# The second product of a decoder MLP by one level of Strassen's rule, in a phase of its own behind the first product

## The chip, the cores and the metric

The kernel runs on one core of a Trainium2 chip, in one launch. The metric is the device time of an execution in microseconds (us); three runs of the kernel before took 2086.72, 2089.35 and 2091.54 us, with 2089.35 as their median. A core has TensorE (PE: matrix products, whose weights are loaded by PEld), VectorE (DVE), ScalarE (ACT), GpSimd (POOL), SyncE (SP, which here issues nearly all transfers) and 16 DMA engines between the device memory (DRAM) and the on-chip memory (SBUF). Products are summed in PSUM, eight banks of 128 x 512 numbers.

## The reference

One decoder layer on 512 tokens of 2048 features, in float32. Three mixers share one input projection; the part that matters here is the end:

```python
x = x + gate1 * (concat[A, B, C] @ W_out)
x = x + gate2 * squared-ReLU MLP(adaLN(RMSNorm(x), c))
# A final RMSNorm is applied after the last layer.
D_MODEL = 2048; SEQ = 512; DEPTH = 1; D_FF = 4 * D_MODEL

def rms_norm(x, g):
    xf = x.astype(jnp.float32)
    y = xf * lax.rsqrt(jnp.mean(xf * xf, axis=-1, keepdims=True) + EPS)
    return (y * g.astype(jnp.float32)).astype(x.dtype)
```

The MLP's first product is 512 x 2048 by 2048 x 8192, then ReLU and a square; its second product is 512 x 8192 by 8192 x 2048. gate2 and the scales and shifts of adaLN are products of the vector c with the matrix ada_w.

## The kernel before

Every float32 product is made of float32r parts: each factor is split into a high part (a cast) and a low part (the factor less its high part), and three matmuls (high by high, low by high, high by low) stand for one. A matmul has a 128 x 128 stationary factor and a moving factor of 512 columns, so it yields 128 x 512 numbers.

Weights come as pieces of 128 x 512 (256 KB). The class Stream loads them on SP's queue in the order of use (L91, tile w_raw), ScalarE casts them (L104, w_hi) and VectorE makes the low part (L105, w_lo), three buffers each. The order in which its calls stand sets the order of the work; all queues are in order.

The first product of the MLP has 64 hidden tiles of 128 features by 512 tokens. Tiles 0 to 6 are made at once, with seven PSUM banks, while norm 2 is still under way; each of the other 57 is 16 pieces' worth of matmuls, 48, in four pieces (L258 to L260, ps_m). Behind a tile, hidden() applies ReLU (L852, ACT), squares (L856, DVE) and splits into m_hi (L857, ACT) and m_lo (L858, DVE). During the tiles behind the seventh, x1 (the residual) is transposed block by block (L842), copied (L844, tile x1t, two buffers) and written to x1_dram (x_dram in the profile).

The second product runs along with the first: mlp2(c) takes chunk c of four hidden tiles, two chunks behind mlp1. For each of four column quarters q it does four hidden tiles by four token blocks by three matmuls into four PSUM banks (L900 to L902, ps_d), 192 matmuls per chunk, and VectorE adds each bank into the sums acc (L892; chunk 0 is a copy on ScalarE). Chunk 14 multiplies by gate2 (g2row) and adds x1. The last chunk, mlp2_last, runs token block by token block (ps_e), and behind each block come squares (L937), the final gain (L938), the sum of squares (L940), one over the root with a Newton step (L304 to L310), the scaling (L947 on DVE, L945 on ACT) and the writes to out.

ada_w, 2 x 1024 columns a piece, is dotted with c on VectorE (L211) between other work, up to the first tiles of the MLP; it loads in transfers of 1 MB or 512 KB on the same SP queue.

## Time and profile before

| | |
|---|---|
| runs | 2086.72, 2089.35, 2091.54 us |
| profiled execution's span | 2089.8 us |
| PE busy | 2062.8 us, 99% |
| DVE busy | 1272.5 us, 61% |
| ACT busy | 776.5 us, 37% |
| DMA, mean | 155 GB/s, 323 MB |

The span of the profiled execution is its own time and stands 0.5 us from the median of the runs. Shares of busy time are averages over all stages. TensorE's busy time is modelled from the starts of its matmuls, so 99% says that there is nearly always one under way. Idle time of an engine counts only where TensorE waits for it.

### The profile page before, as it was taken

The page shows a single profiled execution, that of the slowest core. Times are in us where ns is not written, and L with a number is a line of the kernel's source. Part 1 is how long each engine was busy: PE and PEld are TensorE (multiplying, and loading weights), DVE is VectorE, ACT ScalarE, POOL GpSimd, SP SyncE. Part 2 cuts the span into 40 slices and gives each one's busy share as a digit, 9 for nine tenths or more (in the row PEclk, how much of TensorE's full clock was granted, in tenths as well). Part 3 has the DMA queues.
Part 4 walks back from the last instruction along what each step waited for, and adds up shares of the span by engine and source line. Part 5 has one row for each costly group of instructions (what it writes and reads, how often), then busy time and mean ns, then how long its engine had stood idle before and what let it go on. Part 6 is the DMA issues. An engine that isn't in the chain of part 4 may idle for free.

```text
span 2089.8 us, 26292 instructions
## 1 busy us (share of the span) xinstructions
PE 2062.8 (99%) x9525; PEld 1698.8 (81%) x9525; DVE 1272.5 (61%) x2225; ACT 776.5 (37%) x1433; POOL 3.8 (0%) x12
## 2 busy tenths in 40 slices
PE   9999999999999999999999999999999999999998
PEld 7889877778888887888888888888888888888786
DVE  8998878788977973445544434444344443444687
ACT  4435357766323554323222232222322223222323
POOL 0000000000000000000000000000000000000000
PEclk9999999999999999999999999999999999999999
DMA  9895855546894355545333333333333333333552
GB/s 389 285 318 155 256 161 175 177 155 233 301 341 137 94 190 186 155 117 178 120 116 96 96 97 101 96 96 96 97 100 96 96 91 96 97 98 98 152 161 91
DMA packets 145378, 323.44 MB, mean 155 GB/s; under 512 B 16120, under 2 KB 26944, under 8 KB 138720
## 3 DMA queue, kind: packets, MB, share of 16 engines
q1 hardware_dynamic: 143376, 319.00, 48.6%
q10 hardware_dynamic: 1824, 2.65, 0.4%
q8 instruction: 75, 1.23, 0.2%
q14 instruction: 55, 0.45, 0.1%
q0 software_dynamic: 48, 0.11, 0.0%
...
## 4 chain that ended last, share of the span: by engine, by line
PE 92%; DMA 3%; DVE 3%; issue 1%; ACT 1%; SPq 0%; ACTq 0%; DVEq 0%
PE ps_m L258 11%; PE ps_m L260 11%; PE ps_m L259 11%; PE ps_d L900 10%; PE ps_d L901 10%; PE ps_d L902 10%; PE ps_w L259 3%; PE ps_w L258 3%; PE ps_w L260 3%; PE ps_y L258 1%; PE ps_y L259 1%; PE ps_y L260 1%; PE ps_x L258 1%; PE ps_x L259 1%; PE ps_x L260 1%; DMA w_raw<-in_w 1%
## 5 line engine op out<-in xcount | busy, mean ns | idle before, releaser
L105 DVE TENSOR_TENSOR w_lo<-w_raw,w_hi 128x512 fp32r<-128x512 f32 (+2 forms) x732 | 492.7, 676 | 689.1 <-ACT w_hi L104 678.4
L104 ACT CAST w_hi<-w_raw 128x512 fp32r<-128x512 f32 (+2 forms) x732 | 444.9, 610 | 1066.3 <-PE ps_d L902 432.6
L900 PE MATMUL ps_d<-w_hi,m_hi 128*128 128x512 f32 x960 | 374.6, 391 | 4.1 <-DVE acc L892 2.2
L901 PE MATMUL ps_d<-w_lo,m_hi 128*128 128x512 f32 x960 | 374.4, 390 | 0.0
L902 PE MATMUL ps_d<-w_hi,m_lo 128*128 128x512 f32 x960 | 373.7, 390 | 0.0
L258 PE MATMUL ps_m<-h_hi,w_hi 128*128 128x512 f32 x912 | 356.5, 391 | 0.0
L260 PE MATMUL ps_m<-h_hi,w_lo 128*128 128x512 f32 x912 | 355.1, 389 | 0.0
L259 PE MATMUL ps_m<-h_lo,w_hi 128*128 128x512 f32 x912 | 354.8, 389 | 0.0
L211 DVE SCALAR_TENSOR_TENSOR ada<-ada,crow 128x1024 f32<-128x1024 f32 (+1 forms) x176 | 229.5, 1317 | 11.8 <-DMA ada<-in_ada_w 11.3
L900 PEld LDWEIGHTS ps_d<-w_hi,m_hi 128*128 128x128 f32 x960 | 180.6, 188 | 44.6 <-DVE acc L892 2.6
L902 PEld LDWEIGHTS ps_d<-w_hi,m_lo 128*128 128x128 f32 x960 | 180.6, 188 | 37.6
L901 PEld LDWEIGHTS ps_d<-w_lo,m_hi 128*128 128x128 f32 x960 | 180.5, 188 | 37.3 <-DVE w_lo L105 0.2
L260 PEld LDWEIGHTS ps_m<-h_hi,w_lo 128*128 128x128 f32 x912 | 171.2, 188 | 35.9
L258 PEld LDWEIGHTS ps_m<-h_hi,w_hi 128*128 128x128 f32 x912 | 171.2, 188 | 35.2
L259 PEld LDWEIGHTS ps_m<-h_lo,w_hi 128*128 128x128 f32 x912 | 171.3, 188 | 35.1
L892 DVE TENSOR_TENSOR acc<-acc,ps_d 128x512 f32<-128x512 f32 x224 | 139.6, 680 | 1.8 <-PE ps_d L902 1.8
L858 DVE TENSOR_TENSOR m_lo<-m_t,m_hi 128x512 fp32r<-128x512 f32 x64 | 44.2, 691 | 40.7 <-ACT m_hi L857 40.5
L857 ACT CAST m_hi<-m_t 128x512 fp32r<-128x512 f32 x64 | 39.7, 620 | 47.2 <-DVE m_t L856 47.2
L259 PE MATMUL ps_y<-h_lo,w_hi 128*128 128x512 f32 x128 | 50.0, 390 | 0.8 <-DVE h_lo L337 0.8
L259 PE MATMUL ps_w<-mixc_lo,w_hi 128*128 128x512 f32 x128 | 49.9, 390 | 0.0
L260 PE MATMUL ps_y<-h_hi,w_lo 128*128 128x512 f32 x128 | 49.8, 389 | 0.0
L258 PE MATMUL ps_w<-mixc_hi,w_hi 128*128 128x512 f32 x128 | 49.8, 389 | 0.0
...
## 6 DMA issues: line engine op xcount, KB each, us to landing
w_raw<-in_w SPq DMA_DIRECT2D x668, 256.0 KB, 2.7
ada<-in_ada_w SPq DMA_DIRECT2D x50, 1024.0 KB, 7.1
ada<-in_ada_w SPq DMA_DIRECT2D x92, 512.0 KB, 4.8
...
xT<-in_xT SPq DMA_DIRECT2D x16, 256.0 KB, 7.1
qT<-in_w SPq DMA_DIRECT2D x16, 256.0 KB, 2.8
row<-acs_dram SPq DMA_DIRECT2D x16, 256.0 KB, 3.6
xin<-in_xT SPq DMA_DIRECT2D x16, 256.0 KB, 4.5
```

Of the source, the lines that this page charges most:

```text
L104: self.split = nc.scalar.copy(hi, raw)
L105: self.in_order(lambda: nc.vector.tensor_sub(lo, raw, hi.bitcast(F32)))
L211: return V.scalar_tensor_tensor(w, w, 0.5, crow[:, sl], ALU.mult, ALU.mult, accum_out=acc[:, n:n + 1])
L258: PE.matmul(ps, lhsT=wh, rhs=pair[0], start=first, stop=False)
L259: PE.matmul(ps, lhsT=wh, rhs=pair[1], start=False, stop=False)
L260: PE.matmul(ps, lhsT=wl, rhs=pair[0], start=False, stop=last)
L857: S.copy(hi, t)
L858: V.tensor_sub(lo, t, hi.bitcast(F32))
L892: V.tensor_add(dst, dst, banks[t])
L900: PE.matmul(ps, lhsT=hid[0][:, ts], rhs=w[0], start=first, stop=False)
L901: PE.matmul(ps, lhsT=hid[0][:, ts], rhs=w[1], start=False, stop=False)
L902: PE.matmul(ps, lhsT=hid[1][:, ts], rhs=w[0], start=False, stop=last)
```

## The change

The two products of the MLP become two phases.

In the first phase all 64 hidden tiles are made, one after the other. Hidden tiles n and n + 1 (n even) form a pair; their 512 tokens are cut in halves of 256, which gives the four blocks a11, a21, a12, a22 of Strassen's rule (in Winograd's form). Four subtractions make the other left factors; all seven (128 x 7 x 256) are cast to hx_hi and hx_lo and written to hid_dram, two transfers of 0.92 MB per pair, 64 in all. Only the first product's weights go through Stream here; add_pieces finds where the second product's weights lie in DRAM.

In the second phase the pools of the first are closed. For two column halves p, eight chunks c of four pairs of hidden tiles and seven products m (in the order 2, 4, 3, 6, 5, 1, 7) there is a right factor: a block of weights b11, b21, b22 or b12 (128 x 4 x 512, loaded in two transfers of 512 KB) or one of four sums of blocks, made in place on VectorE. It is split into v_hi and v_lo, and the left factor hs comes back from hid_dram in one transfer of 1 MB. A product is 24 matmuls into a PSUM tile of two banks, of which there are four. VectorE adds it into one of seven sums (128 x 2 x 512). After the eighth chunk the sums are combined into four result blocks, multiplied by gate2, x1 is added, and the final norm follows.

```diff
-        hi = mlp.tile([P, T], F32R, tag="m_hi", bufs=12, name=f"m_hi{f}")
-        lo = mlp.tile([P, T], F32R, tag="m_lo", bufs=12, name=f"m_lo{f}")
-    def mlp2(c, hid):
...
-    def mlp2_last(hid):
...
-    hid = [mlp1(c) for c in range(lead)]
-    for c in range(nchunk - 1):
-        if c + lead < nchunk:
-            hid.append(mlp1(c + lead))
...
-        mlp2(c, hid[c])
-    mlp2_last(hid[-1])
+    for n in range(NFT):
...
+        if n % 2 == 0:
+            x = mlp.tile([P, 7, HT], F32, tag="hx", bufs=2, name=f"hx{n // 2}")
+            relu2(halves(x, 0), ps, cols)
+            continue
+        relu2(halves(x, 5), ps, cols)
+        a11, a21, a12, a22 = x[:, 0], x[:, 1], x[:, 5], x[:, 6]
+        V.tensor_sub(x[:, 2], a12, a22)
+        V.tensor_sub(a12, a12, a11)
+        V.tensor_sub(x[:, 3], a22, a12)
+        V.tensor_sub(x[:, 4], a21, x[:, 3])
+        hi = mlp.tile([P, 7, HT], F32R, tag="hx_hi", bufs=2, name=f"hx_hi{n // 2}")
+        lo = mlp.tile([P, 7, HT], F32R, tag="hx_lo", bufs=2, name=f"hx_lo{n // 2}")
+        S.copy(hi, x)
+        V.tensor_sub(lo, x, hi.bitcast(F32))
+        for part, y in enumerate((hi, lo)):
+            nc.sync.dma_start(hid_dram[n // (2 * KP)][:, :, part, n // 2 % KP].rearrange("i p t -> p i t"), y.bitcast(F32))
...
+    order = (2, 4, 3, 6, 5, 1, 7)
+    def right_factors(p, c):
+        b = []
+        for i, k in enumerate(("11", "21", "22", "12")):
+            b.append(w2_tile(f"b{k}_{p}_{c}"))
+            for half in range(2):
...
+                nc.sync.dma_start(b[-1][:, 2 * half:2 * half + 2], w)
+            if i < 3:
+                yield b[-1]
+        b11, b21, b22, b12 = b
+        q = w2_tile(f"q{p}_{c}")
+        V.tensor_add(q, b11, b12)
+        yield q
+        V.tensor_add(b12, b12, b22)
+        yield b12
+        V.tensor_add(b11, b11, b12)
+        yield b11
+        V.tensor_add(b21, b21, b11)
+        yield b21
...
+                    hs = hs_pool.tile([P, 2, KP, HT], F32R, tag="hs", bufs=3, name=f"hs{p}_{c}_{i}")
+                    nc.sync.dma_start(hs.bitcast(F32), hid_dram[c][i])
+                    hi = wp.tile([P, KP, T], F32R, tag="hi", bufs=3, name=f"v_hi{p}_{c}_{i}")
+                    lo = wp.tile([P, KP, T], F32R, tag="lo", bufs=3, name=f"v_lo{p}_{c}_{i}")
+                    S.copy(hi, raw)
+                    V.tensor_sub(lo, raw, hi.bitcast(F32))
...
+        for k in range(KP):
+            PE.matmul(ps, lhsT=hs[:, 0, k, ts], rhs=hi[:, k], start=(k == 0), stop=False)
+            PE.matmul(ps, lhsT=hs[:, 1, k, ts], rhs=hi[:, k], start=False, stop=False)
+        for k in range(KP):
+            PE.matmul(ps, lhsT=hs[:, 0, k, ts], rhs=lo[:, k], start=False, stop=(k == KP - 1))
...
+    ahead = [next(todo), next(todo)]
+    for _ in range(2 * NCK * 7):
+        p, c, m, hs, hi, lo = ahead.pop(0)
...
+        if c == 0:
+            sums[m] = late.tile([P, 2, T], F32, tag="sum", bufs=11, name=f"sum{p}_{m}")
+            S.copy(sums[m], ps)
+        else:
+            add(sums[m], ps)
...
+        if m == 4:
+            add(sums[7], sums[4])
+            add(sums[4], sums[2])
+            residual(1, 2 * p, sums[4])
+            squares(1, 2 * p)
...
+        elif m == 1:
+            add(sums[7], sums[1])
+            add(sums[6], sums[1])
+            residual(1, 2 * p + 1, sums[6])
+            squares(1, 2 * p + 1)
+            if p:
+                for t in range(2):
+                    write_out(1, t)
+                residual(0, 2, sums[7])
```

residual() multiplies a result block of 128 x 1024 by gate2 and adds x1 (two VectorE operations, L1003 and L1004), squares() makes two squares on ScalarE and two products with the final gain on VectorE (L1012), and write_out() does what stood behind a token block before. In the second column half the last product m = 7 is followed token block by token block.

Three places show how the change moves the work. In the rows a name ends in a running number; of v_lo0_4_6 the figures are column half, chunk and slot of the left factor, of ps_d0_4_2 column half, chunk and product.

VectorE in the middle of the second product, before (chunk 8, where it alternates between splitting weights and adding PSUM banks):

```order
L105 TENSOR_TENSOR w_lo534_13089<-w_raw_534_13086,w_hi534_13088 128x512
L105 TENSOR_TENSOR w_lo535_13107<-w_raw_535_13104,w_hi535_13106 128x512
L105 TENSOR_TENSOR w_lo536_13125<-w_raw_536_13122,w_hi536_13124 128x512
L105 TENSOR_TENSOR w_lo537_13143<-w_raw_537_13140,w_hi537_13142 128x512
L892 TENSOR_TENSOR acc2_7898<-acc2_7898,ps_d8_2_0_13082 128x512
L892 TENSOR_TENSOR acc2_7898<-acc2_7898,ps_d8_2_1_13083 128x512
L892 TENSOR_TENSOR acc2_7898<-acc2_7898,ps_d8_2_2_13084 128x512
L892 TENSOR_TENSOR acc2_7898<-acc2_7898,ps_d8_2_3_13085 128x512
```

The same place in the changed kernel (column half 0, chunk 4):

```order
L984 TENSOR_TENSOR v_lo0_4_1_12934<-b11_0_4_12928,v_hi0_4_1_12933 128x2048
L964 TENSOR_TENSOR q0_4_13036<-b11_0_4_12928,b12_0_4_13033 128x2048
L1029 TENSOR_TENSOR sum0_1_12237<-sum0_1_12237,ps_d0_3_1_12937 128x1024
L984 TENSOR_TENSOR v_lo0_4_6_12969<-b21_0_4_12963,v_hi0_4_6_12968 128x2048
L966 TENSOR_TENSOR b12_0_4_13033<-b12_0_4_13033,b22_0_4_12998 128x2048
L1029 TENSOR_TENSOR sum0_7_12273<-sum0_7_12273,ps_d0_3_7_12972 128x1024
L984 TENSOR_TENSOR v_lo0_4_5_13004<-b22_0_4_12998,v_hi0_4_5_13003 128x2048
L968 TENSOR_TENSOR b11_0_4_12928<-b11_0_4_12928,b12_0_4_13033 128x2048
L1029 TENSOR_TENSOR sum0_2_12061<-sum0_2_12061,ps_d0_4_2_13007 128x1024
L984 TENSOR_TENSOR v_lo0_4_4_13041<-q0_4_13036,v_hi0_4_4_13040 128x2048
L970 TENSOR_TENSOR b21_0_4_12963<-b21_0_4_12963,b11_0_4_12928 128x2048
L1029 TENSOR_TENSOR sum0_4_12099<-sum0_4_12099,ps_d0_4_4_13044 128x1024
```

Operations are four times as long, and additions that make right factors (q, b12, b11, b21) stand between the splits and the sums.

SP's queue where the last weights of the first product are loaded, before (nothing but weights):

```order
L91 DMA w_raw_679_16008<-in_w 128x512
L91 DMA w_raw_680_16026<-in_w 128x512
L91 DMA w_raw_681_16044<-in_w 128x512
L91 DMA w_raw_682_16070<-in_w 128x512
L91 DMA w_raw_683_16088<-in_w 128x512
L91 DMA w_raw_684_16106<-in_w 128x512
```

The same place in the changed kernel, where the phases meet:

```order
L125 DMA w_raw_474_11920<-in_w 128x512
L919 DMA hid_dram7_7129<-hx_hi30_11837 128x7x256
L125 DMA w_raw_475_11938<-in_w 128x512
L919 DMA hid_dram7_7129<-hx_lo30_11838 128x7x256
L959 DMA b11_0_0_12009<-in_w 128x2x512 x2
L959 DMA b21_0_0_12018<-in_w 128x2x512
L919 DMA hid_dram7_7129<-hx_hi31_11986 128x7x256
L919 DMA hid_dram7_7129<-hx_lo31_11987 128x7x256
L959 DMA b21_0_0_12018<-in_w 128x2x512
L959 DMA b22_0_0_12027<-in_w 128x2x512 x2
L959 DMA b12_0_0_12063<-in_w 128x2x512 x2
L980 DMA hs0_0_4_12068<-hid_dram0_7122 128x2048
```

The loads of the first group's weights b21, b22 and b12 stand behind the writes of the last pair's left factors (hx_hi31, hx_lo31).

VectorE at the end of the program, before (the last token block):

```order
L935 TENSOR_TENSOR acc3_7979<-acc3_7979,ps_e3_3_17268 128x512
L938 TENSOR_TENSOR acc3_7979<-acc3_7979,frow_14227 128x512
L940 TENSOR_REDUCE fin3_17212<-fin3_17212 128x1
L304 TENSOR_SCALAR fin3_17212<-fin3_17212 128x1
L306 RECIPROCAL fin3_17212<-fin3_17212 128x1
L307 TENSOR_TENSOR fin3_17212<-fin3_17212 128x1
L308 TENSOR_TENSOR fin3_17212<-fin3_17212 128x1
L309 TENSOR_SCALAR fin3_17212<-fin3_17212 128x1
L310 TENSOR_TENSOR fin3_17212<-fin3_17212 128x1
L947 TENSOR_SCALAR acc0_7736<-acc0_7736,fin3_17212 128x512
L947 TENSOR_SCALAR acc2_7898<-acc2_7898,fin3_17212 128x512
```

In the changed kernel, from the sum of the last product but one on (46 rows end the program from there; these are the first):

```order
L1029 TENSOR_TENSOR sum1_1_14243<-sum1_1_14243,ps_d1_7_1_15924 128x1024
L1003 TENSOR_TENSOR sum1_3_14139<-sum1_3_14139,g2row_13480 128x1024
L1029 TENSOR_TENSOR sum1_7_14279<-sum1_7_14279,sum1_1_14243 128x1024
L1004 TENSOR_TENSOR sum1_3_14139<-sum1_3_14139,x1in0_3_15914 128x1024
L1029 TENSOR_TENSOR sum1_6_14173<-sum1_6_14173,sum1_1_14243 128x1024
L1012 TENSOR_TENSOR sum1_3_14139<-sum1_3_14139,frow_13501 128x512 x2
L1003 TENSOR_TENSOR sum1_6_14173<-sum1_6_14173,g2row_13480 128x1024
L1003 TENSOR_TENSOR sum1_7_14279<-sum1_7_14279,g2row_13480 128x1024
L1004 TENSOR_TENSOR sum1_6_14173<-sum1_6_14173,x1in1_3_15952 128x1024
L1004 TENSOR_TENSOR sum1_7_14279<-sum1_7_14279,x1in0_2_15994 128x1024
L1012 TENSOR_TENSOR sum1_6_14173<-sum1_6_14173,frow_13501 128x512 x2
L1017 TENSOR_REDUCE fin_12008<-fin_12008 128x1 x2
```

What was spread over four token blocks now stands behind the last two products.

## Rows read from the trace of the kernel before

**Rows 1.** The page's head: span, busy time by engine, TensorE's clock in 40 slices.
```profile
span 2089.8 us, 26292 instructions
...
PE 2062.8 (99%) x9525; PEld 1698.8 (81%) x9525; DVE 1272.5 (61%) x2225; ACT 776.5 (37%) x1433; POOL 3.8 (0%) x12
...
PEclk9999999999999999999999999999999999999999
```
**Rows 2.** By line, TensorE: operation, shapes, count | busy us, mean ns | idle before.
```profile
L900 PE MATMUL ps_d<-w_hi,m_hi 128*128 128x512 f32 x960 | 374.6, 391 | 4.1 <-DVE acc L892 2.2 <-ACT x1t L844 1.8
```
**Rows 3.** Timeline of TensorE in the MLP: start us, us, operation.
```profile
1394.98 0.39 PE L258 MATMUL ps_m<-h_hi,w_hi 128*128 128x512 f32 x1
...
1397.70 0.39 PE L258 MATMUL ps_m<-h_hi,w_hi 128*128 128x512 f32 x1
```
**Rows 4.** By line and shape, VectorE and ScalarE, the whole span.
```profile
L752 DVE TENSOR_TENSOR xs<-xs,ps_rms_c 128x2048 f32<-128x2048 f32 x2 | 4.6, 2285 | 1.9 <-PE ps_rms_c L321 1.9
...
L211 DVE SCALAR_TENSOR_TENSOR ada<-ada,crow 128x1024 f32<-128x1024 f32 x160 | 192.9, 1220 | 11.7 <-DMA ada<-in_ada_w 11.3
...
L462 DVE SCALAR_TENSOR_TENSOR gva<-gva,va 128x256 f32<-128x256 f32 x8 | 3.2, 419 | 0.0
...
L104 ACT CAST w_hi<-w_raw 128x512 fp32r<-128x512 f32 x668 | 414.5, 621 | 1017.4 <-PE ps_d L902 432.6 <-PE ps_m L259 379.4 <-PE ps_w L259 81.9
...
L104 ACT CAST w_hi<-w_raw 128x384 fp32r<-128x384 f32 x48 | 24.5, 511 | 36.3 <-PE ps_m L259 11.1 <-PE ps_tm L502 8.2 <-issue 6.0
...
L852 ACT ACTIVATE m_t<-ps_m 128x512 f32<-128x512 f32 x57 | 33.7, 591 | 0.0
...
L844 ACT COPY x1t<-ps_x1t 128x512 f32<-128x512 f32 x16 | 9.3, 584 | 12.5 <-DMA x_dram<-x1t 12.4
```
**Rows 5.** Timeline of VectorE in the beginning of the MLP.
```profile
745.61 0.68 DVE L856 TENSOR_TENSOR m_t<-m_t 128x512 f32<-128x512 f32 x1
746.21 0.69 DVE L854 TENSOR_TENSOR m_t<-ps_m,r 128x512 f32<-128x512 f32 x1
...
763.49 1.22 DVE L211 SCALAR_TENSOR_TENSOR ada<-ada,crow 128x1024 f32<-128x1024 f32 x1
764.63 0.68 DVE L858 TENSOR_TENSOR m_lo<-m_t,m_hi 128x512 fp32r<-128x512 f32 x1
```
**Rows 6.** Windows: us; PE, PEld, DVE, ACT, POOL busy; PE clock; DMA share; GB/s.
```profile
10.00:20.00 10.00, 10.00 (x33) 8.20 (x33) 9.82 (x18) 4.73 (x9) 0.00 (x0) 1.00 1.04 419
...
785.00:795.00 10.00, 10.00 (x52) 8.21 (x51) 5.86 (x10) 4.08 (x8) 0.00 (x0) 1.00 0.93 301
...
805.00:815.00 10.00, 8.24 (x32) 6.28 (x31) 2.68 (x4) 2.84 (x5) 0.00 (x0) 0.83 0.53 187
...
1000.00:1800.00 800.00, 800.00 (x3546) 662.83 (x3545) 338.92 (x523) 224.83 (x369) 0.00 (x0) 1.00 0.35 99
```
**Rows 7.** DMA issues: out<-in, queue, count, KB each, median us to landing.
```profile
ada<-in_ada_w SPq DMA_DIRECT2D x50, 1024.0 KB, 7.1
ada<-in_ada_w SPq DMA_DIRECT2D x92, 512.0 KB, 4.8
...
x_dram<-x1t SPq DMA_DIRECT2D x16, 256.0 KB, 5.1
```
**Rows 8.** Timeline of TensorE where the transposes of x1 wait.
```profile
809.77 0.50 PE L900 MATMUL ps_d<-w_hi,m_hi 128*128 128x512 f32 x1 [1.76 <-ACT x1t L844]
```
**Rows 9.** Timeline of TensorE and VectorE at the end of the span.
```profile
2079.99 0.39 PE L902 MATMUL ps_e<-w_hi,m_lo 128*128 128x512 f32 x1
...
2083.55 0.16 DVE L308 TENSOR_TENSOR fin<-fin 128x1 f32<-128x1 f32 x1
2083.75 0.15 DVE L309 TENSOR_SCALAR fin<-fin 128x1 f32<-128x1 f32 x1
...
2084.13 0.88 DVE L947 TENSOR_SCALAR acc<-acc,fin 128x512 f32<-128x512 f32 x2
```

More of the change, by code (lines that the diff above doesn't have):

```diff
@@ L63, with add_pieces, up, up4 @@
 ROW, ROW_N = _slots([("dt_bias", 16), ("a_log", 16), ("attn_sinks", 16), ("gm_bs", 512)])
+def add_pieces(stream, sizes):
+    offs = [0]
+    for n in sizes:
+        offs.append(offs[-1] + n * P)
+    count = [0, {}]
+    def up(n):
+        for _ in range(n):
+            stream.add(sizes[count[0]], offs[count[0]])
+            count[0] += 1
+    def up4(c):
+        up(4 * len(range(max(7, 4 * c), 4 * c + 4)))
+    def down(c):
+        for q in range(4):
+            for f in range(4 * c, 4 * c + 4):
+                count[1][q, f] = offs[count[0]]
+                count[0] += 1
+    last = NFT // 4 - 1
+    up(len(sizes) - 4 * (NFT - 7) - 4 * NFT)
+    up4(0)
+    up4(1)
+    for c in range(last):
+        if c + 2 <= last:
+            up4(c + 2)
+        down(c)
+    down(last)
+    return count[1]
 def mix_rows():
@@ L899, in mms2 @@
[L899 to L913 removed]
+            V.tensor_mul(dst, ps, r2)
@@ new lines, in prepared @@
+    def prepared():
+        for p in range(2):
+            for c in range(NCK):
+                for m, raw in zip(order, right_factors(p, c)):
+                    i = slot[m]
+                    hs = hs_pool.tile([P, 2, KP, HT], F32R, tag="hs", bufs=3, name=f"hs{p}_{c}_{i}")
[4 more added lines that the diff above has]
+                    V.tensor_sub(lo, raw, hi.bitcast(F32))
+                    yield p, c, m, hs, hi, lo
@@ new lines, in add, with sub @@
+    def add(d, s):
+        V.tensor_add(d, d, s)
+    def sub(d, s):
+        V.tensor_sub(d, d, s)
+    sums = {}
+    todo = prepared()
+    ahead = [next(todo), next(todo)]
+    for _ in range(2 * NCK * 7):
+        p, c, m, hs, hi, lo = ahead.pop(0)
+        if (p, c, m) == (0, NCK - 2, order[0]):
+            g2row, frow = final_rows()
+        ahead += [x for x in (next(todo, None),) if x]
+        ps = psum.tile([P, 2, T], F32, tag="m", bufs=4, name=f"ps_d{p}_{c}_{m}")
+        last = c == NCK - 1
+        for t in range(2):
+            product(ps[:, t], hs, hi, lo, t)
+            if last and p and m == 7:
+                d = sums[7]
+                y = late.tile([P, T], F32, tag="sq", bufs=2, name=f"fin_y{t}")
+                V.tensor_mul(y, ps[:, t], g2row[:, 2])
+                V.tensor_add(d[:, t], d[:, t], y)
+                squares(0, 2, (t,))
+                write_out(0, t)
+        if last and p and m == 7:
+            break
+        if c == 0:
+            sums[m] = late.tile([P, 2, T], F32, tag="sum", bufs=11, name=f"sum{p}_{m}")
+            S.copy(sums[m], ps)
+        else:
+            add(sums[m], ps)
+        if not last:
+            continue
+        if m == 4:
[3 more added lines that the diff above has]
+            squares(1, 2 * p)
+        elif m == 6:
+            add(sums[6], sums[3])
+            sub(sums[6], sums[2])
+        elif m == 5:
+            sub(sums[7], sums[5])
+            add(sums[3], sums[5])
+            residual(0, 2 * p + 1, sums[3])
+            squares(0, 2 * p + 1)
+        elif m == 1:
[4 more added lines that the diff above has]
+            if p:
+                for t in range(2):
+                    write_out(1, t)
+                residual(0, 2, sums[7])
+        elif m == 7:
+            residual(0, 0, sums[7])
+            squares(0, 0)
```

197 lines of the change are left out of this document (86 added, 111 removed).

## The prediction

> **What bounds the kernel now.** I read the head of the page first: TensorE is busy 2062.8 of 2089.8 us [rows 1], and its clock row shows the high level in all 40 slices [rows 1]. The view by line comes next: the second product's 960 matmuls of the first part waited 4.1 us altogether, 2.2 of that for VectorE's additions into acc [rows 2]. So the time is the number of matmuls by their pitch, plus what lies ahead of the first and behind the last. The pitch stands in the timeline: two matmuls 12 places apart start at 1394.98 and 1397.70, so 2.72 / 12 = 0.2267 us (the 0.39 in the rows is one matmul's passage, pipelined with the next) [rows 3]. I then looked at what each helper has to spare, since the change trades matmuls for work on VectorE, ScalarE and the DMA queues.
>
> **Removed.** Before, the second product has 16 chunks of 192 matmuls, 3072. After, 2 column halves by 8 chunks by 7 products of 24 matmuls, 2688. The size of each (128x512) stays, so 384 x 0.2267 = **-87.0 us**. The 2.2 us of waiting for acc goes too: four PSUM buffers of two banks stand between a product and its sum: **-2.2**.
>
> **Added: VectorE in the second phase.** A product lasts 24 x 0.2267 = 5.44 us, a group of seven 38.1, all 16 groups 609 (against 696 before). VectorE gets seven subtractions and four additions of 128x2048 and seven sums of 128x1024 per group. Their durations: 2285 and 1220 ns [rows 4]. Behind one another they cost less: 128x512 operations of 0.68 start 0.60 apart, and the next starts 1.14 after one of 1.22 [rows 5]; so I take 2.20 (an estimate, 2.285 less the same 0.08) and 1.14. A group is 11 x 2.20 + 7 x 1.14 = 32.2 of 38.1 us. ScalarE casts 128x2048 seven times: 128x384 took 511 ns and 128x512 621 [rows 4], a slope of 0.86 ns an element, so about 1.94 us (an estimate), 13.6 us per group. Both are prepared two products ahead in three buffers, so TensorE covers them: **0**. What it costs if the cover fails is rival B.
>
> The Trainium skill ("VectorE: DVE Perf Modes", section "The DRAIN you can't avoid") says that VectorE's next operation does not start before the pipe of the one ahead is empty. The rows disagree here, with starts 0.60 apart for 0.68 us [rows 5]. By the rule a group would be 33.7 us, still inside 38.1, and the ends worked out below some 3 us longer, which would give 2037.
>
> **Added: DMA.** Phase 2 reads 112 left factors of 1.05 MB and 67 MB of weights, 184.5 MB in 609 us: 303 GB/s. The queues carried 419 GB/s at full share in 10 to 20 us and 301 at 0.93 in 785 to 795 [rows 6]; in the MLP 99 GB/s took a share of 0.35, which is 285 GB/s at full share if it scales [rows 6]. These bounds lie on both sides of 303. I take the high one, as rows of 2 and 8 KB (like those loads of ada_w) are what phase 2 moves: **0**. A left factor is asked for when its buffer's product three places earlier ends, and so has 10.9 us; a 1 MB load landed after 7.1 and 512 KB after 4.8 in the crowded beginning [rows 7]. Phase 1 writes two times 0.92 MB per pair of hidden tiles, 21.8 us, beside eight weight pieces of 0.26 MB: 181 GB/s, below any bound: **0** in its steady part. At its beginning the first eight such writes fall where ada_w still loads and shares reach 0.93 [rows 6]; there the write of x1 (12.4 us of waiting for it at L844 [rows 4]) had already held TensorE 1.76 us [rows 8], after which a stretch of ten microseconds had TensorE busy for 8.24 at a granted clock of 0.83, between its two levels, 1.2 and 2.4 GHz [rows 6]. Bounds: this stall goes (-3.5, the 1.76 and the slower clock behind it), or the eight writes are exposed at their 7.4 MB / 301 GB/s = 25 us. I take **+3**, near the stall that is there already.
>
> **Added: the boundary of the phases.** Clock from the end of the last matmul of phase 1: ReLU 0.59 [rows 4], square 0.60, four subtractions of 128x256 at 419 ns [rows 4] to about 3.1; cast of 128x1792 by the slope above, 1.72, to 4.9. The cast of the right factor of the first group's second weight quarter stands behind it on ScalarE (its place is that of the last hidden operand): 6.8 with its 1.94. TensorE's preloaded first product covers nothing before its own right factor is split, whose place comes free at 0 as well; so TensorE idles about 6.9 us. On SP the second half of b21 and all of b22 and b12 stand behind the two writes of the last pair, which wait until 4.9 and 6.9; b21 lands about 13, b22 16, b12 18 (0.5 to 1 MB each at 300 to 400 GB/s). Behind that, four additions and the splits follow at VectorE's pace, and the first group ends about 47.5 instead of 38.1: **+10**, with 7 (only the idle) and 20 (loads at a third of the speed and TensorE at its lower clock behind them) as bounds.
>
> **Added: change of the column half.** The last group of the first half carries extra sums, residuals and squares on VectorE: 8 of 128x1024 for sums and 8 for residuals, 8 of 128x512, 16 x 1.14 + 8 x 0.60 = 23 us on top of 32.2, in 38.1 us. That is 17 too much; two products ahead (10.9) and the slack of the next group (5.9) take it nearly up. I take **+5**, as the splits stand between these in one in-order queue; bounds 0 and 12.
>
> **The end.** Before, the last matmul starts at 2079.99 and the span ends 2089.8: 9.4 us behind PE's end [rows 9]. After, count from the last group's first product's end; the products end every 5.44, the one before the last at 27.2, the last at 32.6. VectorE keeps pace until 27.2 and then has (the order's rows from sum1_1 on) nine operations of 128x1024 at 1.14 (10.3), ten of 128x512 at 0.60 (6.0), eight scalings of 0.44 (0.88 for two) [rows 9] (3.5) and 28 tiny ones at 0.19 (2083.55 to 2083.75) [rows 9] (5.3): 25.1, to 52.3. The last scaling ended 2085.0 before and the span 4.8 later [rows 9]: 57.1, so 24.5 us behind PE's end: **+15** (12 if the small ones overlap, 22 if VectorE is already late at 27.2).
>
> **Sum.** -87.0 - 2.2 + 3 + 10 + 5 + 15 = -56. The profiled execution's span of 2089.8 equals the median of the runs (2089.35) within 0.5 us, so I take 2089.8 - 56 = **2034 us**. With all low bounds (-3.5, 7, 0, 12) it is 2016, with all but the exposed writes at their high ones (3, 20, 12, 22) 2058.
>
> **Rivals.**
> A. *The queues bound phase 2.* At the 285 GB/s of the MLP [rows 6], 184.5 MB take 647 us, 38 more than 609: 2072. For: that rate is from the same weights in the same 2 KB rows. Against: a share scaled up is not a rate seen, and 394 to 419 were. Slower than before only below about 278 GB/s. 15%.
> B. *TensorE waits for the right factors.* This one ends on the other side. The cast, the subtraction and the additions of one product are a chain (b11 needs b12, b21 needs b11), and VectorE's in-order queue puts a sum, which waits for the end of a product, between them. If each product then exposed its cast and the lost overlap, a group lasts 7 x (5.44 + 1.1) = 45.8 us, 16 groups 733: 2034 + 123 = 2157. The point from which it decides: a group above 38.1 + 56 / 16 = 41.6 us. With VectorE merely taking 40 us, +30: 2064. For: VectorE is at 85% with in-order waits. Against: the two-product lead of 10.9 us against a longest VectorE block of 2.20 + 2.20 + 1.14 = 5.5. 10% for the version that is slower, 8% for that at 2064.
> C. *The writes of the left factors in 1 KB rows fill the queues in phase 1.* They are 58.7 MB; if they moved at a third of 301 GB/s, a pair's 1.84 MB would take 18.4 of its 21.8 us and its 2.1 MB of weights another 7.0: 3.6 us over by 28 pairs, +101: 2135, slower. Against: no row shows a write so slow; x1's 256 KB landed after 5.1 us in the median on a crowded queue [rows 7]. 3%.
> The forecast holds the other 64%.
>
> **How the numbers follow.** About 0.2% is what a measurement of this kernel tells from no change, 4 us. Faster: the forecast 64, A 14 of 15, the mild B 8: 86%. Slower: B 10, C 2, a bit of A: 12%. Within: 2%. The forecast's own range is 2016 to 2058; A and the mild B, at 2064 and 2072, are taken in: 2015 to 2075, and left out is some 17%.
>
> **What would show it.** 2688 matmuls in the second phase at 0.227 us and a granted clock at its high level bear out the first term. In the first stretch of ten microseconds of phase 2 TensorE should be busy for some 3, its idle put down to the cast of a right factor and to DMA b22 or b12. In the steady part a group should repeat every 38.1 us, with VectorE busy 33 of it and DMA near 300 GB/s. If its matmuls wait there for v_lo, it is B; if they wait for hs or the raw weights, A; if matmuls of the first product wait for w_lo with DMA named behind, C. Behind the last matmul some 24 us of VectorE should stand. Wrong it is altogether if the group takes over 41.6 us.

## The result, and the profile after

The changed kernel took 2040.49 us (median of four runs, 2036.87 to 2043.13) where the kernel before, in the same session, took 2088.70: a ratio of 0.9765 with the interval 0.9751 to 0.9778, 48 us less. Forecast were 2034 in a range of 2015 to 2075. The profiled execution's span is 2041.4, so the two profiles differ by 48.4 us, and the terms below are counted on them.

The page's head after it, for [rows 1]: TensorE has 79 us less to do, VectorE 265 more, and the clock row shows its first lower slice at the very end.

```profile
span 2041.4 us, 25012 instructions
...
PE 1983.8 (97%) x9141; PEld 1628.7 (80%) x9141; DVE 1537.5 (75%) x2086; ACT 847.8 (42%) x1253; POOL 3.8 (0%) x12
...
PEclk9999999999999999999999999999999999999997
```

The second product's matmuls, for [rows 2] and [rows 3]. By line, the first group of matmuls (L991) now waits 21.0 us, all of it in five waits at the three seams shown below. In the timeline two blocks of 12 matmuls start 2.72 us apart, 0.2267 each as before, and two groups of seven products 38.08 apart.

```profile
L991 PE MATMUL ps_d<-v_hi,hs 128*128 128x512 f32 x896 | 351.3, 392 | 21.0 <-DVE fin L337 10.8 <-ACT v_hi L983 10.2
```
```profile
1436.28 0.39 PE L991 MATMUL ps_d<-v_hi,hs 128*128 128x512 f32 x1
...
1474.36 0.39 PE L991 MATMUL ps_d<-v_hi,hs 128*128 128x512 f32 x1
...
1991.34 0.39 PE L991 MATMUL ps_d<-v_hi,hs 128*128 128x512 f32 x1
...
1994.06 0.39 PE L991 MATMUL ps_d<-v_hi,hs 128*128 128x512 f32 x1
```

Windows (columns as in [rows 6]). In 150 us of the changed kernel's steady second phase TensorE never waits; VectorE is busy for 132 of them, ScalarE for 53, and the DMA engines carry 316 GB/s at a share of 0.87. The beginning of the MLP, 760 to 940, is where TensorE loses 8.6 us with the DMA engines at 0.90. The first line below is the kernel before's for that stretch, the other two are the changed kernel's.

```profile
760.00:940.00 180.00, 178.24 (x807) 146.79 (x806) 85.19 (x135) 66.84 (x114) 0.00 (x0) 0.99 0.55 170
```
```profile
760.00:940.00 180.00, 171.41 (x763) 138.78 (x762) 117.08 (x186) 67.57 (x101) 0.00 (x0) 0.98 0.90 296
```
```profile
1450.00:1600.00 150.00, 150.00 (x664) 124.20 (x663) 132.21 (x74) 52.93 (x28) 0.00 (x0) 1.00 0.87 316
```

TensorE's timeline at the three seams: between the phases (the last matmul of the first phase, then the waits of the first group), where the column halves meet, and at the end. A wait stands in brackets.

```profile
1387.56 0.39 PE L293 MATMUL ps_m<-h_hi,w_lo 128*128 128x512 f32 x1
1394.72 0.80 PE L991 MATMUL ps_d<-v_hi,hs 128*128 128x512 f32 x1 [6.77 <-ACT v_hi L983]
...
1402.99 0.50 PE L991 MATMUL ps_d<-v_hi,hs 128*128 128x512 f32 x1 [0.80 <-ACT v_hi L983]
...
1405.32 1.20 PE L994 MATMUL ps_d<-v_lo,hs 128*128 128x512 f32 x4 [0.21 <-DVE v_lo L984]
...
1720.46 1.20 PE L994 MATMUL ps_d<-v_lo,hs 128*128 128x512 f32 x4 [1.15 <-DVE v_lo L984]
...
1725.73 0.50 PE L991 MATMUL ps_d<-v_hi,hs 128*128 128x512 f32 x1 [1.36 <-ACT v_hi L983]
...
1729.14 0.50 PE L991 MATMUL ps_d<-v_hi,hs 128*128 128x512 f32 x1 [1.29 <-ACT v_hi L983]
...
2012.19 1.07 PE L994 MATMUL ps_d<-v_lo,hs 128*128 128x512 f32 x4
2024.07 0.80 PE L991 MATMUL ps_d<-v_hi,hs 128*128 128x512 f32 x1 [10.81 <-DVE fin L337]
```

Behind the two long waits the matmuls are slower: from 1394.72 and from 2024.07 they start 0.43 apart for 3.6 us at least, and the granted clock of 1395 to 1398 is 0.50, the lower of the two levels. Behind the waits of 1.15 to 1.36 us where the halves meet it stays at the upper level:

```profile
1395.00:1398.00 3.00, 3.00 (x8) 2.33 (x9) 2.13 (x1) 0.00 (x0) 0.00 (x0) 0.50 1.09 386
1719.00:1732.00 13.00, 9.20 (x38) 6.71 (x37) 13.00 (x9) 6.06 (x7) 0.00 (x0) 1.00 0.90 327
```

Two rows of ScalarE name what TensorE's waits for v_hi hang on. At the boundary the cast of the second right factor waits for the load of b21; where the halves meet, the cast of q waits for VectorE, which has no gap between 1694 and 1733.

```profile
1401.03 1.91 ACT L983 CAST v_hi<-b 128x2048 fp32r<-128x2048 f32 x1 [6.36 <-DMA b<-in_w]
...
1723.78 1.91 ACT L983 CAST v_hi<-q 128x2048 fp32r<-128x2048 f32 x1 [0.80 <-DVE q L964]
```

VectorE's timeline at the end, for [rows 9]: from the sum of the last product but one it has no gap until 2028.15, and its last scaling starts at 2035.55. In the kernel before, one token block's work stood there.

```profile
2010.58 1.22 DVE L1029 TENSOR_TENSOR sum<-sum,ps_d 128x1024 f32<-128x1024 f32 x1
2011.72 1.22 DVE L1003 TENSOR_TENSOR sum<-sum,g2row 128x1024 f32<-128x1024 f32 x1
...
2029.60 0.69 DVE L1050 TENSOR_TENSOR fin_y<-ps_d,g2row 128x512 f32<-128x512 f32 x1 [1.44 <-PE ps_d L994]
...
2035.55 0.88 DVE L1025 TENSOR_SCALAR sum<-sum,fin 128x512 f32<-128x512 f32 x2
```

### The profile page after: what moved, and what is told of

The parts are those of the page before. It is cut to its first block, busy times and chain, and to the rows that moved or that the text cites. A ratio compares the mean times of both kernels' runs of the same rounds, so it can differ in the third digit from the quotient of the medians.

```text
span 2041.4 us, 25012 instructions
## 1 busy us (share of the span) xinstructions
PE 1983.8 (97%) x9141; PEld 1628.7 (80%) x9141; DVE 1537.5 (75%) x2086; ACT 847.8 (42%) x1253; POOL 3.8 (0%) x12
## 4 chain that ended last, share of the span: by engine, by line
PE 84%; DVE 8%; DMA 5%; issue 1%; ACT 1%; SPq 0%; ACTq 0%; DVEq 0%
PE ps_m L293 11%; PE ps_m L291 11%; PE ps_m L292 11%; PE ps_d L994 9%; PE ps_d L991 9%; PE ps_d L992 9%; PE ps_w L292 3%; PE ps_w L291 3%; PE ps_w L293 3%; DMA ada<-in_ada_w 1%; PE ps_y L291 1%; PE ps_y L292 1%; PE ps_y L293 1%; DVE sum L1029 1%; DVE ada L246 1%
## 5 line engine op out<-in xcount | busy, mean ns | idle before, releaser
L135 ACT CAST w_hi<-w_raw 128x512 fp32r<-128x512 f32 (+2 forms) x476 | 284.9, 603 | 586.2 <-PE ps_m L292 331.5
L136 DVE TENSOR_TENSOR w_lo<-w_raw,w_hi 128x512 fp32r<-128x512 f32 (+2 forms) x476 | 316.0, 668 | 271.3 <-ACT w_hi L135 263.7
L991 PE MATMUL ps_d<-v_hi,hs 128*128 128x512 f32 x896 | 351.3, 392 | 21.0 <-DVE fin L337 10.8
L992 PE MATMUL ps_d<-v_hi,hs 128*128 128x512 f32 x896 | 350.5, 391 | 0.0
L983 ACT CAST v_hi<-b 128x2048 fp32r<-128x2048 f32 x96 | 183.6, 1915 | 304.4 <-PE ps_d L992 229.0
L246 DVE SCALAR_TENSOR_TENSOR ada<-ada,crow 128x1024 f32<-128x1024 f32 (+1 forms) x176 | 230.9, 1320 | 40.0 <-DMA ada<-in_ada_w 39.6
L994 PE MATMUL ps_d<-v_lo,hs 128*128 128x512 f32 x896 | 240.7, 390 | 1.4 <-DVE v_lo L984 1.4
L984 DVE TENSOR_TENSOR v_lo<-b,v_hi 128x2048 fp32r<-128x2048 f32 x96 | 219.4, 2287 | 15.6 <-ACT v_hi L983 15.6
L991 PEld LDWEIGHTS ps_d<-v_hi,hs 128*128 128x128 f32 x896 | 169.2, 189 | 58.2 <-ACT v_hi L983 11.9
L994 PEld LDWEIGHTS ps_d<-v_lo,hs 128*128 128x128 f32 x896 | 168.8, 189 | 37.4 <-DVE v_lo L984 2.2
L992 PEld LDWEIGHTS ps_d<-v_hi,hs 128*128 128x128 f32 x896 | 169.3, 189 | 35.1
L1029 DVE TENSOR_TENSOR sum<-sum,ps_d 128x1024 f32<-128x1024 f32 x97 | 118.2, 1218 | 61.8 <-PE ps_d L994 61.8
L917 DVE TENSOR_TENSOR hx_lo<-hx,hx_hi 128x1792 fp32r<-128x1792 f32 x32 | 64.8, 2025 | 31.4 <-ACT hx_hi L916 31.4
L983 ACT CAST v_hi<-q 128x2048 fp32r<-128x2048 f32 x16 | 30.6, 1915 | 49.9 <-PE ps_d L992 42.5
```

The source lines that it names most:

```text
L135: self.split = nc.scalar.copy(hi, raw)
L136: self.in_order(lambda: nc.vector.tensor_sub(lo, raw, hi.bitcast(F32)))
L246: return V.scalar_tensor_tensor(w, w, 0.5, crow[:, sl], ALU.mult, ALU.mult, accum_out=acc[:, n:n + 1])
L983: S.copy(hi, raw)
L984: V.tensor_sub(lo, raw, hi.bitcast(F32))
L991: PE.matmul(ps, lhsT=hs[:, 0, k, ts], rhs=hi[:, k], start=(k == 0), stop=False)
```

## The experiments

Times are medians; the kernel before took 2088.2 to 2089.8 in the sessions, and the executions of one kernel spread by 1.3 to 6.3 us, so medians of four compare to about 2 us. For smaller steps the profiles help: from the start of the last matmul of phase 1 to the end of the span it is 653.8, 653.6 and 653.8 us in the three kernels with the same second phase (the changed one and experiments 2 and 11). This stretch is called "phase 2 with its end" below; each figure is of one execution. "The changed kernel" is the 2040.49 above.

**1. The first half's residuals later.** Result blocks of the first column half are multiplied by gate2, added to x1 and squared two groups later.

```diff
-            residual(1, 2 * p, sums[4])
-            squares(1, 2 * p)
+            finish(p, 1, 2 * p, sums[4])   # p = 0: put on a list
...
+            if p and c > 1 and later:
+                later.pop(0)()
```

> The residuals and squares of the first column half (8 operations of 128x1024 and 8 of 128x512 on VectorE, about 14 us) are emitted two groups later, where VectorE has some 6 us to spare per group. Theory (VectorE is overloaded where the column halves meet): the waits of TensorE there, 3.8 us in three places plus about 0.9 us of slower clock, shrink to 0 to 1.5 us, and the time falls by 3 to 5 us to about 2036. Rival (the first group of the second half waits for its weights, whose loads are late on SP's queue): the three waits stay within 1 us of 3.8 and the time stays at 2040.

Measured: 2034.44, ratio to before 0.9737 (0.9721 to 0.9752). All three waits at the meeting of the halves are gone from TensorE's timeline. From the last matmul of phase 1 to the end of the last product, without its PSUM wait, it is 623.3 us and not 627.9, so 4.6 us came from there (about 0.6 of it at the boundary, where the wait for b21 happened to be 0.23 and not 0.80); the rest is spread ahead of phase 2. The edit also moves the loads of x1 off SP's queue at that place, so that it does not by itself part the two sides; the rows above do, with VectorE without a gap and ScalarE's cast waiting for it. VectorE's overload was the cause.

**2. The last pieces of ada_w later.**

```diff
-            full_k(ps, h2, (4, 12) if n == 7 else (4,), x1_tokens if n > 7 else None)
+            full_k(ps, h2, (4,) if n > 24 else (), x1_tokens if n > 7 else None)
```

> The last 16 pieces of ada_w (gate2) are loaded and dotted behind hidden tile 24 and not from tile 7 on. Theory (the beginning of the MLP is crowded: VectorE's in-order queue holds the splits of weights behind dots that wait for late pieces of ada_w): between 760 and 940 us TensorE's idle time falls from 8.6 us to 1 to 3, VectorE's waits for ada_w fall from 39.6 us to under 15, and the time falls by 5 to 9 us to 2031 to 2035. Rival (the writes of the left factors and of x1 alone hold SP's queue): the idle time there stays above 6 us and the time within 2 us of 2040.

Measured: 2030.03, 0.9719 (0.9704 to 0.9733), the largest gain of a single edit, 10.5 us where 5 to 9 were expected. The window, to be held against the changed kernel's above: idle 1.5 us in place of 8.6, and a DMA share of 0.67. VectorE's waits for ada_w fell from 39.6 to 11.2 us.

```profile
760.00:940.00 180.00, 178.46 (x813) 146.51 (x812) 87.45 (x129) 71.33 (x105) 0.00 (x0) 1.00 0.67 221
```

The expectation blamed VectorE's in-order queue. The edit moves the bytes, the dots and the waits for late pieces together, so its time does not part them; experiment 11 takes out the dots' work. The trace of the changed kernel shows the queue in all three stalls for w_lo. In this one the cast of the weight was done at 856.71, but its split stood behind a dot that waited 3.77 us for its piece; in the other two (895.31 and 922.99) it stands behind hx_lo and dots that had waited as well.

```profile
859.50 1.23 DVE L246 SCALAR_TENSOR_TENSOR ada<-ada,crow 128x1024 f32<-128x1024 f32 x1 [3.77 <-DMA ada<-in_ada_w]
...
860.65 1.29 DVE L136 TENSOR_TENSOR w_lo<-w_raw,w_hi 128x512 fp32r<-128x512 f32 x2
...
861.40 0.50 PE L293 MATMUL ps_m<-h_hi,w_lo 128*128 128x512 f32 x1 [1.95 <-DVE w_lo L136]
```

**3. All writes of left factors on GpSimd's queue.**

```diff
-            nc.sync.dma_start(hid_dram[n // (2 * KP)]...
+            nc.gpsimd.dma_start(hid_dram[n // (2 * KP)]...
```

> All 64 writes of left factors are issued on GpSimd's queue and not on SP's. Theory for the boundary of the phases (the loads of the first group's weights stand behind writes that wait for the last pair's split): b21 lands before its cast is due, the second product starts without its wait, the first group takes 38 to 39.5 us instead of 41.6, and the idle time ahead of it stays at 6.8 us, since the cast stands behind the last hidden operand on ScalarE. Rival (VectorE's pace sets the first group): it stays at 41 us or more. For the beginning of the MLP: if the order on SP's queue is at fault, its 8.6 us of idle time fall to under 4; if the bytes are, they stay above 6. Time 2031 to 2038 by the theory, 2040 by the rival.

Measured: 2049.35, 0.9806 (0.9788 to 0.9824): 9 us slower than the changed kernel, which neither side expected. At the boundary the second product waits no more, after the same 6.77 us, but the first group took 40.5 us and not the 38 to 39.5 expected, since its slow matmuls behind the long wait stay. In the beginning TensorE was idle for 11.7 us of 760 to 940 at a mean clock of 0.97, and the last matmul of phase 1 started at 1395.97 and not at 1387.56. Its waits there now name the cast of a weight (6.8 us for w_hi) and its low part (4.7), no more the transposes. ScalarE's waits for weights rose from 25.9 to 65.8 us in this window, while VectorE's for ada_w fell from 34.0 to 6.3. So in this kernel it is the weights that come late, and not VectorE's queue that holds them up. The likely reason is that on SP's queue the writes had stood in line with the weights and now compete with them for the DMA engines; no run shows that by itself.

```profile
760.00:940.00 180.00, 168.29 (x730) 133.16 (x729) 112.46 (x180) 65.18 (x99) 16.95 (x18) 0.97 0.83 291
```

**4. VectorE's splits twice.**

```diff
                     V.tensor_sub(lo, raw, hi.bitcast(F32))
+                    V.tensor_sub(lo, raw, hi.bitcast(F32))
```

> Every low part of a right factor (v_lo, 128x2048) is made twice, which changes no number and adds 7 x 2.20 = 15.4 us of VectorE per group: 32.2 becomes 47.6. Theory (the phase is the larger of TensorE's 38.1 and VectorE's sum, in-order waits cost little): steady groups take 47 to 49 us and the span grows by 140 to 165 us to about 2190. Rival (VectorE's in-order queue exposes a part of the chain of every product, as in rival B of the prediction): groups of 52 us or more, over 2250.

Measured in one run: 2209.86, span 2208.2, 166.8 more than the changed kernel. A steady group takes 47.7 us (the two rows of TensorE below are one group apart) where VectorE's sum is 47.6, and VectorE is busy for 99.8 of 100 us. The phase follows the larger of the two sums, and waits in the in-order queue cost next to nothing. Of the growth, 16 x 9.65 = 154 us is that; the other 12 fall outside the steady groups, and the whole is 2 us above the upper end expected.

```profile
1600.00:1700.00 100.00, 88.88 (x384) 70.83 (x384) 99.81 (x54) 28.37 (x16) 0.00 (x0) 0.97 0.66 236
```
```profile
1615.74 1.34 PE L995 MATMUL ps_d<-v_lo,hs 128*128 128x512 f32 x4 [2.49 <-DVE v_lo L985]
...
1663.48 1.32 PE L995 MATMUL ps_d<-v_lo,hs 128*128 128x512 f32 x4 [2.48 <-DVE v_lo L985]
```

**5. Two PSUM tiles for the last product.**

```diff
+            if last and p and m == 7 and t:
+                ps = psum.tile([P, 2, T], F32, tag="m", bufs=4, name=f"ps_d{p}_{c}_{m}_b")
             product(ps[:, t], hs, hi, lo, t)
```

> The two token blocks of the last product get a PSUM tile each. Theory (the end is VectorE's backlog of 25 us; TensorE's 10.8 us of waiting there for a bank that VectorE still has to read is only its shadow): TensorE's wait goes, its last matmul moves from 2029 to about 2016, and the time falls by only 1 to 2.5 us, to about 2038.5. Rival (the wait is on the path): the time falls by about 10 us to 2030.

Measured: 2039.33, 0.9765 (0.9750 to 0.9780): the wait of 10.81 is gone, the last four matmuls start at 2012.68 and not at 2027.65, and the time moved by 1.2, which the runs do not tell from nothing. Phase 2 with its end did not get shorter in the profile (655.2 and not 653.8). The longest wait that TensorE has in the changed kernel is worth at most a tenth of its length: VectorE was behind in any case.

**6. Sums combined a chunk earlier.** With the two PSUM tiles and one Newton step for two token blocks.

```diff
+        elif last:
+            for op, i in uses[m]:          # 12 additions straight into results
+                op(sums[i], ps)
+        if c == NCK - 2:
+            if m == 4:
+                add(sums[7], sums[4])
+                add(sums[4], sums[2])
...
```

> In both column halves the eight sums that combine products are made in the chunk before the last, the last chunk's products go straight into the results (12 additions in place of 15), the two token blocks of the upper half share one Newton step, and the last product has two PSUM tiles. Theory (the 25 us behind TensorE's end are VectorE's backlog, each operation worth its own time): of nine, ten and 28 operations behind the last product but one, eight, ten and 21 are left, 2.5 us less, and with the PSUM tile's 1.2 us and up to 1 us at the change of halves the time falls by 3 to 5 us to 2035 to 2037. Rival (the end hangs on the last block's own chain of square, root and write): not more than the 1.2 us of the two tiles alone.

Measured: 2043.10, 0.9784 (0.9769 to 0.9798): no gain, 2.6 us more by the medians. In the profiles phase 2 with its end is 657.3 us, against 655.2 with the two PSUM tiles alone: the end (last product's end to span's end) shortened from 27.0 to 24.9 us, but the products ended 4.1 later. At the end VectorE now waited 2.31 us for a root on ScalarE, which stood behind scalings. TensorE got new waits in the last chunk of each half:

```profile
1691.04 0.50 PE L991 MATMUL ps_d<-v_hi,hs 128*128 128x512 f32 x1 [0.49 <-ACT v_hi L983]
...
1694.36 0.50 PE L991 MATMUL ps_d<-v_hi,hs 128*128 128x512 f32 x1 [1.21 <-ACT v_hi L983]
...
2002.24 0.50 PE L991 MATMUL ps_d<-v_hi,hs 128*128 128x512 f32 x1 [0.50 <-ACT v_hi L983]
...
2005.56 0.50 PE L991 MATMUL ps_d<-v_hi,hs 128*128 128x512 f32 x1 [1.21 <-ACT v_hi L983]
```

Eight more sums (9.1 us) in a group with 5.9 us to spare are waited for in the group behind it, and what they took off the end is less than that.

**7. The boundary.** The last pair alone is written from GpSimd's queue, its high part copied by VectorE.

```diff
-        S.copy(hi, x)
+        (V.tensor_copy if n == NFT - 1 else S.copy)(hi, x)
...
+            (nc.gpsimd if n == NFT - 1 else nc.sync).dma_start(hid_dram[n // (2 * KP)]...
```

> The last pair's left factors alone are written from GpSimd's queue, and their high part is copied by VectorE, so that ScalarE is free for the first right factor. Theory for the boundary (loads behind writes on SP, cast behind cast on ScalarE): the idle time ahead of the first product falls from 6.8 to 2.5 to 4 us, the waits of the second product for b21 (0.8 and 0.2 us) go, but the low part of the first right factor now stands behind two operations of 128x1792 on VectorE, at about 9 us, so that part of the gain comes back as a wait of the first product for v_lo; together 1 to 3 us less, 2037.5 to 2039.5. Rival (the bytes of the writes collide with the loads, whatever the queue): no change at the second product.

Measured: 2038.61, 0.9769 (0.9750 to 0.9788), 1.9 us less by the medians; phase 2 with its end is 1.1 shorter (652.7). The idle time fell from 6.77 to 2.47, and 2.68 came back as the wait for v_lo, as expected:

```profile
1387.14 0.80 PE L991 MATMUL ps_d<-v_hi,hs 128*128 128x512 f32 x1 [2.47 <-ACT v_hi L983]
...
1393.31 1.89 PE L994 MATMUL ps_d<-v_lo,hs 128*128 128x512 f32 x4 [2.68 <-DVE v_lo L984]
```

**8. All of 1, 2, 5, 6 and 7.**

> All of it together: the first column half's residuals later, the last 16 pieces of ada_w behind tile 24, sums combined a chunk earlier, one Newton step for two token blocks, two PSUM tiles for the last product, the last pair's writes on GpSimd's queue. If the terms are separate, as the theory has them (beginning 10, change of halves 4 to 5, end 3 to 4, boundary 1 to 3): 18 to 22 us less than 2040, so 2018 to 2023. Rival (what is saved in one place is waited for in the next, since VectorE is at 85% in every group): over 2027.

Measured: 2026.64, 0.9705 (0.9691 to 0.9720), between what the two sides expected; the earlier sums were kept in it, as experiment 6 had run in the same session.

**9. Without the earlier sums (1, 2, 5 and 7).**

> Four of the edits without the sums combined a chunk earlier and without the shared Newton step: the first column half's residuals later, the last 16 pieces of ada_w behind tile 24, two PSUM tiles for the last product, the last pair's writes on GpSimd's queue with VectorE's copy. Theory (the earlier combining overloaded VectorE in the chunk before the last and cost 4 us there while it saved less than 1 behind TensorE's end): the terms that held alone add up, 6 + 10 + 1 + 2, about 2021 to 2024, at least 2 us below the 2026.6 with it. Rival (the sums are not to blame): 2026 to 2028.

Measured: 2024.87 (five runs), 0.9692 (0.9675 to 0.9710). The new waits in the last chunk are gone, but 1.8 us of difference to the kernel with them is within what sessions differ by: by time alone this is open. The profiles, one each, side with the theory: from the end of phase 1 to the end of the last product it is 621.3 us and not 625.0, behind that 26.7 and not 25.4, so that the earlier sums cost 3.7 and saved 1.3.

**10. GpSimd takes part of the end.**

```diff
-        V.tensor_add(d, d, xin)
+        eng.tensor_add(d, d, xin)      # G for two of the last four result blocks
...
-            V.tensor_mul(d[:, t], d[:, t], frow[:, q])
+            eng.tensor_mul(d[:, t], d[:, t], frow[:, q])
```

> As the one before, and GpSimd, idle otherwise, adds x1 to two of the last four result blocks and multiplies them by the final gain (2 of 128x1024, 4 of 128x512, 4.7 us on VectorE). Theory (the end is VectorE's backlog): 3 to 5 us less than the kernel without it, 2017 to 2020. Rival (GpSimd is so slow, or slows VectorE so much by reading the same memory, that its share ends last): no gain or a loss.

Measured: 2027.76, 0.9704 (0.9686 to 0.9722), 2.9 us slower than the same kernel without it (experiment 9, same session). VectorE has fewer operations, but where they meet GpSimd's, one of the two is slower: of the first meeting below VectorE's split keeps its time and GpSimd's addition takes 4.31 us where its later one takes 2.40; at the second, VectorE's operations are the slower ones. GpSimd's share does not end last (at 2001.95). That the slowed operations are the whole of the loss is not shown. Timelines of both engines, with GpSimd, then VectorE without it:

```profile
1978.89 2.28 DVE L984 TENSOR_TENSOR v_lo<-b,v_hi 128x2048 fp32r<-128x2048 f32 x1
1979.12 4.31 POOL L1004 TENSOR_TENSOR sum<-sum,x1in 128x1024 f32<-128x1024 f32 x1 [596.20 <-DVE sum L1003]
...
1996.17 4.66 DVE L1029 TENSOR_TENSOR sum<-sum,sum 128x1024 f32<-128x1024 f32 x2
2000.75 3.41 DVE L1003 TENSOR_TENSOR sum<-sum,g2row 128x1024 f32<-128x1024 f32 x2
...
1995.13 2.40 POOL L1004 TENSOR_TENSOR sum<-sum,x1in 128x1024 f32<-128x1024 f32 x1 [8.20 <-issue]
1998.37 3.58 POOL L1012 TENSOR_TENSOR sum<-sum,frow 128x512 f32<-128x512 f32 x2 [0.83 <-ACT fin_q L1011]
```
```profile
1996.08 2.35 DVE L1003 TENSOR_TENSOR sum<-sum,g2row 128x1024 f32<-128x1024 f32 x2
1998.35 2.36 DVE L1004 TENSOR_TENSOR sum<-sum,x1in 128x1024 f32<-128x1024 f32 x2
```

**11. Dots without their loads.**

```diff
-                t = groups.tile([P, 1024], F32, tag="ada", bufs=2, name=f"ada{n}_{i}")
-                nc.sync.dma_start(t, a["ada_w"][n][:, sl])
+                if mlp_on and i in again:
+                    t = again[i]
```

> The changed kernel, in which the last 16 pieces of ada_w are dotted at the same places as in it, but on one piece that stays in memory: 30 loads of 512 KB are left out, and gate2 is not that of the reference. It parts two causes that the later loads took away together. Theory (bytes: the queues carry 296 GB/s at a share of 0.90 between 760 and 940 us, and weights come late): TensorE's idle time there falls from 8.6 us to 1 to 3 and the time to 2030 to 2034, as with the later pieces. Rival (VectorE's work: 32 dots of 1.14 us among the splits): more than 5 us of idle time stay, and the time is 2036 to 2040.

Measured: 2029.95, 0.9716 (0.9698 to 0.9734), as in experiment 2 (2030.03). VectorE does 30 dots in the window, as in the changed kernel (121.88 us busy, more than there), and TensorE loses 1.3 us: the loads were the cause, not the dots' own work. As no dot waits for a late piece any more either, this run does not part weights that come late from a VectorE queue that late pieces hold.

```profile
760.00:940.00 180.00, 178.66 (x813) 146.72 (x812) 121.88 (x192) 73.02 (x108) 0.00 (x0) 1.00 0.72 244
```

**12. The very last chunk plain.** Experiment 9, with the last chunk of the second half as eight products, two per result block in one PSUM tile; a12 of that chunk is kept as an eighth left factor.

```diff
+    residual(1, 2, sums[4])
+    plain(r12, True)
...
+    plain(r12, False)
+    result(1, 2, r12)
...
+        product(ps[:, t], *g[3:], t, True, False)
+        product(ps[:, t], *h[3:], t, False, True)
```

> As the kernel with four edits (2024.9), and the very last chunk of the second column half is not done by Strassen's rule but as eight plain products of two per result block, summed in PSUM: one product more on TensorE (24 matmuls, +5.44 us), but no additions of weights, four splits in place of seven and one addition per result block in place of up to three sums; x1 and gate2 are worked into the sums ahead. Theory (what stands behind TensorE's end is VectorE's work on the sums of the last products, in line): the time behind the last matmul falls from 26.7 to 10 to 14 us, in sum 7 to 11 us less, 2014 to 2018. Rival (the same work, being only moved ahead by some microseconds, is late all the same, since the last two groups together hold about 83 us of VectorE for 82 of TensorE): 18 us or more behind the last matmul, 2021 or more.

Measured: 2017.37 (five runs, 2016.07 to 2019.56), 0.9656 (0.9643 to 0.9669): 7.5 us less than experiment 9 and 23 less than the changed kernel, the fastest here. The last four matmuls start at 2003.61 and the span ends at 2017.8: 13.3 us behind TensorE's end where there were 26.7, paid for with one product. The edit also leaves out the additions of weights and three of seven splits in the last group, so it does not part the sums from these.

```profile
2003.61 1.07 PE L1016 MATMUL ps_r<-v_lo,hs 128*128 128x512 f32 x4
```

## Why the prediction was right, and where its terms were off

The terms on the two profiles, in us. The MLP's first phase goes from the first product of tile 7 on (744.1 before, 745.8 after) to its last matmul (1387.56, end about 1387.95), 642.2; before, the same stretch, to 2080.4, less 3072 x 0.2267 and the 3.6 of gate2's transposes, is 636.3.

| term | forecast | measured | from |
|---|---|---|---|
| 384 matmuls fewer | -87.0 | -87.0 | 2.72 per 12, before and after |
| steady phase 2 | 0 | 0 | groups of 38.08 |
| beginning of the MLP, with the wait for acc | +0.8 | +5.9 | 642.2 less 636.3 |
| boundary | +10 | +10.2 | 6.77, and 41.56 less 38.08 |
| change of halves | +5 | +4.7 | 3.8 of waits, 0.9 of restarts behind them |
| end | +15 | +16.2 | 25.6 less 9.4 |
| ahead of the MLP | 0 | +1.7 | 745.8 less 744.1 |
| sum | -56 | -48.3 | spans: -48.4 |

The end is counted from where the last product would have ended without its wait, 2015.8.

- *Removed.* Exact. Four PSUM buffers did take away the wait for acc.
- *VectorE in phase 2.* The group stays TensorE's. The estimates of 2.20 and 1.94 us held: the splits start 2.20 apart where nothing lies between them, and the cast of 128x2048 took 1915 ns by line. Rival B was refuted, and experiment 4 puts its point: with 47.6 us of VectorE a group took 47.7.
- *DMA in phase 2.* 316 GB/s at a share of 0.87 is 363 at full share if it scales, above the 285 of rival A and below the 419 that I took; 1600 to 1610 carried 365 at a share of 1.01. In the steady part TensorE waited for no hs and no raw weight. Rival C is out for the steady part of phase 1, where 1000 to 1300 us showed no idle time.
- *Beginning of the MLP*, the step that was mis-sized: "I take +3, near the stall that is there already". It cost 5.9 with the 2.2 counted in, so 8.1 in place of the 3; 1.3 to 2.1 of that may belong to this execution, as the same first phase took 640.1 to 640.9 us, and not 642.2, in experiments 1, 5, 6 and 7. The 0.92 MB writes, beside the loads of ada_w, brought the share of 760 to 940 us from 0.55 to 0.90, and six stalls (5.0 us for w_lo, 3.6 for the transposes of x1) came where there had been one. Experiment 11 shows that it is the loads in that stretch and not the work of the dots. Without them (experiments 2 and 11) the first phase takes 630.5 to 630.7 us, less than the 636.3 before, so that the kernel before had lost time in its like stretch too. How late loads reach TensorE differs: in the changed kernel the stalls for w_lo stand behind dots that wait in VectorE's queue, in experiment 3 the weights themselves are late. The prediction also misread a row: the 8.24 us of TensorE in 805 to 815 are not behind the wait of 1.76, they are the ten microseconds that hold it.
- *Boundary.* As worked out, with the cause shown by experiment 7. TensorE was busy for 3.2 of the ten microseconds from 1387 on (forecast: some 3), and the cast of the second right factor started at 1401.03, 13.1 us behind the end of phase 1 (forecast: b21 lands about 13). The loads behind the last writes show as 1.0 us of TensorE's waits (0.80 and 0.21). Of the rest of the first group's 3.5, about 1.9 is the slower clock (12 matmuls in 4.59 us where 2.72 is the pace) and the remainder the restarts behind the two waits, where the first matmul takes 0.50 and the next starts 0.34 behind it. The group ended 48.3 us after the last matmul of phase 1 (1436.28) where the forecast had 47.5.
- *Change of halves.* The cause, VectorE's overload, is right, but that the size came out is in part luck: the prediction's own sum, 17 less 10.9 and 5.9, leaves 0.2, and the +5 was a judgement on top of it. Experiment 1's expectation put 0.9 us down to a slower clock; the granted clock there is 1.00, and the 0.9 are such restarts behind three waits.
- *End.* 1 us over: VectorE's work from the sum of the last product but one to its last scaling took 25.9 us (2010.58 to 2036.43, two waits of 1.44 and 1.04 in it) where the forecast had 25.1. Experiment 5 shows that TensorE's wait there is a shadow, experiment 12 that VectorE's work in line behind the last products makes the length.
- The rule weighed in the prediction, that VectorE starts nothing before the pipe is empty (the Trainium skill, "VectorE: DVE Perf Modes", section "The DRAIN you can't avoid"), was taken there without its limit: the same section says that a next operation that is not held starts earlier. The rows agree with the limit: operations of 1.22 us start 1.14 apart (2010.58, 2011.72). The 2037 us that the rule without it would have given are nearer to the result, but the 3 us are not where the time was lost.

What stays open: by which of the two ways, late weights or VectorE's queue, most of the beginning's time is lost; why the writes on GpSimd's queue make the weights late; and why the MLP's first phase starts between 742.1 and 745.9 in kernels that do the same ahead of it.
